# The end of a decoder layer's last product: a part order, four early weight parts, eight copies on another queue, and scalings behind a tanh

## The chip, the cores and the metric

The kernel runs on one core of a Trainium2 chip. The metric is device time of one execution in microseconds (us), the median of three runs. Engines are named as the profile names them: PE (TensorE, the matrix products), DVE (VectorE), ACT (ScalarE), POOL (GpSimd) and SP (SyncE, which here only issues transfers). SP, ACT and POOL each issue transfers on a queue of their own; the profile writes these issues as SPq, ACTq and POOLq.

## The reference

One layer of a decoder on 512 positions of width 2048, in float32. What matters for the change is its projection and its end:

```python
h = rms_norm(x, norm_g)
proj = h @ w_in                       # q, k, v, gates, u, v, z, merge logits
o_a = nsa_attention(...) * silu(z_a)  # sparse attention
o_b = spatial_gating(...) * silu(z_b)
g_a, g_b = split(sigmoid(merge_logits))
merged = g_a * (o_a @ w_up_a) + g_b * (o_b @ w_up_b)
x = x + merged @ w_out
x = x + sigmoid(x @ w_ple_gate) * (p @ w_ple)
return rms_norm(x, final_g)           # x * rsqrt(mean(x*x) + eps) * final_g
```

## The kernel before

**Products.** A large product is cut in 2 x 2 blocks and made with seven half-size products (numbered 1 to 7) of sums of blocks, not eight. Every float32 operand is split in a high and a low part, and a product of two such operands is three matmuls. The weights' high part is a cast on ACT (`high`, L181: `hs`), the low part a subtraction on DVE (`low`, L187: `ls`), and both go to rings of three tiles of 128x1024. A job is one such product on 512 columns of the weight (and the 512 that lie 1024 further on). It runs part after part; a part, written 70 or 43, is a product's number and a quarter of its depth, and it is 12 matmuls on a 128x512 weight tile. The order of the parts of the last two products (`w_out`: jobs `wo0`, `wo1`; `w_ple_gate`: jobs `pg1`, `pg0`) is a list written by hand (`LATE`).

**Around a part.** `gemm` runs for each part: first what was put off (`flush`, the list `deferred`), then `split_to`, which splits the weights one to three parts ahead (`job.lead` says how far in `pg0`) and issues the next loads, then the functions that the job's plan has for this part (`plan("pg0", 14, ...)`), then the matmuls. So every engine's order of work is the order in which this Python emits it; no scheduler moves anything.

**The last job, `pg0`.** Its parts stand in the order 10 to 13, 20, 21, 50 to 53, 22, 23, 60 to 63, 30 to 33, 70 to 73, 40 to 43. Product 4 is done by rows: for each of two row tiles t all of 40 to 43 (24 matmuls), on top of product 7's sums in PSUM, which must be copied out (L930, `keep<-ps_pg`) before product 4's first matmul overwrites them. In the profiled run part 73 is followed by product 4's first matmul at 1508.88 us. Weights of 72, 40 and 43 are split in tiles of their own (`part_place`: h0, l0, and `ob_h`); 41, 42 and 73 go through the rings.

After a block of the product comes the gate: a tanh on ACT (L970, or L1055 for product 4), `ple_add` on DVE (L963, L965), a square on ACT (L975, L1058, L1065) that adds up the rows' squares. The final norm is a multiplication by `final_g` (`weigh_x2`, L999, DVE; the weights of `final_g` are loaded by `load_fg`) and by each row's inverse root. For rows 0 and 1 the roots come from small steps on DVE (L1004 to L1010) and POOL (L1017 to L1020), for row 2 from a chain of small steps on DVE (L1004 to L1032), for row 3 from ACT's square root (after a table load at L1064). `put` scales a 128x512 block by the root (ACT L1039 for "s", DVE L1041 for "v") and sends it out (L1044).

**The merge stage** (440 to 760 us) makes the merge logits, product by product (`ps_m`), while its plan runs the gating of mixer B in `background` items (`group(g)`, eight of them). In `spatial` each group issues on ACT's queue a copy of 1 MB of `w_out` from DRAM to DRAM (`out_copies`, L1567), and on POOL's queue `add_out` adds another 1 MB to the copy before (L1522). The transfers issued by SP and ACT share eight semaphores in turn, and an engine does not issue a transfer before the transfer that had its semaphore last has landed. The logits' gate goes to DRAM from ACT (L791).

Of the kernel before, what the change touches and what calls it, by code (L numbers as in the profile page):

```python
# [13 lines left out]
F32 = mybir.dt.float32  # L14
# [24 lines left out]
class Job:  # L39
# [8 lines left out]
    def __init__(self, name, kind, w, c0, cols, kt, act, evac, banks=None, tail=0, c2=None,  # L48
                 pairs=("15", "63", "7", "24"), after=None, made=None, order=None, grown=None,
                 seq=None, adds="", lead={}):  # L50
        self.name, self.kind, self.w, self.c0, self.cols, self.kt = name, kind, w, c0, cols, kt
        self.pairs, self.after, self.made, self.order = pairs, after, made, order
        self.grown, self.plan, self.adds, self.lead = grown, {}, adds, lead
# [50 lines left out]
def kernel(ctx: ExitStack, tc: tile.TileContext, x, p, norm_g, w_in,  # L104
# [243 lines left out]
    def split_to(i, more=1):  # L348
        while state["high"] < len(subs):
            h = state["high"]  # L350
            job, k, n, ld = subs[h]
            if h > (i if job.kind == "S" else i + more):
                break
            sum_to(h)
            if job.tail and (k, n) in f_tiles:
                hi = f_tiles[k, n][:, 0:2]
            elif job.kind == "S":
                hi = quad["pool"].tile([P, 2, job.cols], F32R, tag="hs", name="hs", bufs=3)
            else:
                hi = stream.tile([P, n, job.cols], F32R, tag="hi", name="hi", bufs=4)  # L360
            src = source(h)
            {0: nc.vector.tensor_copy, 6: nc.gpsimd.tensor_copy}.get(h, high)(hi, src)
            parts[h] = [hi, None, src]
            state["high"] += 1
        sum_to(i + 1)
        while state["low"] <= min(i, len(subs) - 1):
            job, k, n, ld = subs[state["low"]]
            pt = parts[state["low"]]
            if job.tail and (k, n) in f_tiles:
                pt[1] = f_tiles[k, n][:, 2:4]  # L370
            elif job.kind == "S":
# [20 lines left out]
    def gemm():  # L392
        si = 0
        for job in jobs:
            if job.kind == "S":
# [572 lines left out]
    def gate_x2(p, cg, t, sg, src, soon=True):  # L968

        nc.scalar.activation(sg, src, AF.Tanh, scale=0.5)  # L970

        put_off = soon if callable(soon) else deferred.append if soon else later

# [3 lines left out]
        def second():  # L977
            sl = ple_add(cg, t, sg, pieces[p][t % 2])
            (soon if callable(soon) else deferred.append)(partial(square, sl))
        put_off(second)  # L980

    def final_pg(p, cg, row, ts=(0, 1)):
        other = {"3": "6", "7": "5", "2": "1"}[p]
        for t in ts:
            o = kept[other][t]
            f = partial(gate_x2, p, cg, row + t, o, o)
            if p == "3" and cg == 2:
                behind.append(partial(f, soon=behind.append))
            elif p != "2":
                (deferred.append if cg % 2 == 0 or p == "7" else later)(f)  # L990
# [55 lines left out]
    def put_row(t):  # L1046
        for cg, how in ((1, "s"), (2, "v"), (3, "s"), (0, "v")):
            put(cg, t, how=how)

    def fourth_pg(cg, t, ps):  # L1050
# [5 lines left out]
        sl = ple_add(cg, t, sg, pieces["4"][t % 2])  # L1056
        if t < TT - 1:
            nc.scalar.activation(sg, sl, AF.Square, accum_out=ss[:, t, 0:1])  # L1058
            add_squares(t, t + 1)
            inverse_root(t)  # L1060
# [463 lines left out]
    def group(g):  # L1524
# [25 lines left out]
        def second():  # L1550
            grab("z", zb_dram, "g1", 1)

        def spatial():
# [788 lines left out]
    def part_place(p, j, o):  # L2342
        f_tiles[p, j] = o()
# [55 lines left out]
```

## Time and profile before

| | |
|---|---|
| median of 3 runs | 1536.24 us (1534.26 to 1537.6) |
| the profiled execution: its own time | 1538.38 us |
| its span, first to last instruction | 1536.7 us |
| mean granted TensorE clock | 0.993 |
| PE busy | 1503.3 us (98%) |
| DVE, ACT, POOL busy | 1214.3, 854.3, 350.7 us |

The span is what the trace shows; 1.7 us of the execution's time lie around it. PE is busy nearly all the time, so only two kinds of place are of interest: the few where PE has nothing to do, and the stretch after PE's last matmul. In a timeline row, the first number is the start in us, the second the busy time, and the bracket is the engine's idle time before the row and what ended it.

### The profile page before, as it was taken

Reading aid. Unit: us, or ns where it says so; the run is one execution under the profiler, and the core shown is the slowest. Engines: PE = TensorE matmul, PEld = TensorE weight load, DVE = VectorE, ACT = ScalarE, POOL = GpSimd, SP = SyncE. Lnnn points to the kernel's source line nnn. Section 1 sums busy time; section 2 is a strip of 40 time slices with the busy share of each in tenths; the row PEclk is TensorE's granted clock in tenths of the full one; section 3 lists DMA queues with packets and bytes.
Section 4 is the critical chain, followed back from the end, with each engine's and each line's share of the span. In section 5 each row is a group of like instructions: output and inputs, shape, how many; then the busy total and the mean of one; then the engine's idle time right before and its main releaser. Section 6 shows DMA issues by size and latency. Waiting matters only on the chain.

```text
span 1536.7 us, 20290 instructions
## 1 busy us (share of the span) xinstructions
PE 1503.3 (98%) x7174; PEld 1252.3 (81%) x7174; DVE 1214.3 (79%) x1792; ACT 854.3 (56%) x1423; POOL 350.7 (23%) x507
## 2 busy tenths in 40 slices
PE   9999999999999999999999999999999999999995
PEld 8988888888888888877888888888888878877883
DVE  7787877777888787877578988968988974787677
ACT  6454445444455555544477777765555644555644
POOL 2222343321021212112223342521122111101011
PEclk9999999999999999999999999999999999999998
DMA  8897969673568898979787877678788879668682
GB/s 316 229 301 188 268 110 262 190 233 100 179 196 262 274 280 251 274 249 334 209 178 163 194 177 166 140 188 308 244 274 236 258 176 298 179 209 204 233 246 109
DMA packets 207956, 341.31 MB, mean 222 GB/s; under 512 B 30904, under 2 KB 92000, under 8 KB 206448
## 3 DMA queue, kind: packets, MB, share of 16 engines
q0 software_dynamic: 77856, 129.37, 36.8%
q1 hardware_dynamic: 111296, 161.89, 32.8%
q10 hardware_dynamic: 18704, 48.76, 8.9%
q8 instruction: 56, 0.92, 0.2%
q14 instruction: 44, 0.36, 0.1%
HBM read 284.54 MB, written 106.82 MB: 255 GB/s over the span
## 4 chain that ended last, share of the span: by engine, by line
PE 77%; DVE 8%; DMA 5%; issue 5%; ACT 3%; POOL 1%; ACTq 0%; POOLq 0%; DVEq 0%
PE ps_m L443 4%; PE ps_m L444 4%; PE ps_m L442 4%; PE ps_wo L443 2%; PE ps_wo L442 2%; PE ps_wo L444 2%; DVE ls L187 2%; PE ps_t L1774 2%; PE ps_pg L443 2%; PE ps_pg L442 2%; PE ps_pg L444 2%; PE ps_za L475 2%; PE ps_za L474 2%; PE ps_za L473 2%; PE ps_u L442 2%
## 5 line engine op out<-in xcount | busy, mean ns | idle before, releaser
L187 DVE TENSOR_TENSOR ls<-b,hs 128x1024 fp32r<-128x1024 f32 x160 | 195.8, 1224 | 101.9 <-ACT hs L181 100.8
L181 ACT CAST hs<-b 128x1024 fp32r<-128x1024 f32 x160 | 168.0, 1051 | 193.1 <-PE ps_m L444 53.8
L181 ACT CAST hs<-raw 128x1024 fp32r<-128x1024 f32 x117 | 123.1, 1052 | 132.0 <-PE ps_m L444 27.4
L187 DVE TENSOR_TENSOR ls<-raw,hs 128x1024 fp32r<-128x1024 f32 x117 | 143.2, 1224 | 39.6 <-ACT hs L181 39.2
L187 DVE TENSOR_TENSOR ls<-more,hs 128x1024 fp32r<-128x1024 f32 x94 | 115.0, 1224 | 57.8 <-ACT hs L181 57.6
L181 ACT CAST hs<-more 128x1024 fp32r<-128x1024 f32 x94 | 98.7, 1052 | 96.9 <-PE ps_wo L444 31.6
L442 PE MATMUL ps_m<-hs,act_h 128*128 128x512 f32 x256 | 100.8, 394 | 1.9 <-ACT keep L716 1.9
L443 PE MATMUL ps_m<-ls,act_h 128*128 128x512 f32 x256 | 100.4, 392 | 0.7 <-DVE ls L187 0.7
L444 PE MATMUL ps_m<-hs,act_l 128*128 128x512 f32 x256 | 100.4, 392 | 0.0
L187 DVE TENSOR_TENSOR lo<-raw,hi 128x512 fp32r<-128x512 f32 (+1 forms) x96 | 64.0, 671 | 19.7 <-PE ps_za L475 7.6
L333 DVE TENSOR_TENSOR b<-raw,b 128x1024 f32<-128x1024 f32 x64 | 78.4, 1226 | 0.6 <-DMA raw<-in_w_in_dram 0.6
L333 DVE TENSOR_TENSOR b<-b,b 128x1024 f32<-128x1024 f32 x64 | 78.1, 1220 | 0.1
L1723 ACT ACTIVATE prob<-prob,st 128x512 f32<-128x512 f32 (+3 forms) x128 | 70.8, 560 | 6.0 <-DVE st L1714 6.0
L1714 DVE CUSTOM_DVE_ANT_0 prob<-ps_s,b 128x512 f32<-128x512 f32 (+3 forms) x128 | 56.3, 487 | 13.7 <-PE ps_s L1710 13.5
L181 ACT CAST pth<-ps_t 128x512 fp32r<-128x512 f32 (+1 forms) x88 | 44.1, 547 | 35.0 <-PE ps_t L1774 34.5
L181 ACT CAST hi<-raw 128x512 fp32r<-128x512 f32 (+1 forms) x94 | 54.0, 587 | 15.1 <-PE ps_kw L474 4.0
L442 PEld LDWEIGHTS ps_m<-hs,act_h 128*128 128x128 f32 x256 | 48.5, 189 | 12.3 <-ACT keep L716 2.4
L443 PEld LDWEIGHTS ps_m<-ls,act_h 128*128 128x128 f32 x256 | 48.4, 189 | 11.0 <-DVE ls L187 1.0
L444 PEld LDWEIGHTS ps_m<-hs,act_l 128*128 128x128 f32 x256 | 48.4, 189 | 10.1
L187 DVE TENSOR_TENSOR ptl<-ps_t,pth 128x512 fp32r<-128x512 f32 (+1 forms) x88 | 52.4, 633 | 3.4 <-ACT pth L181 3.4
L473 PE MATMUL ps_za<-act_h,hi 128*128 128x512 f32 x128 | 52.3, 409 | 0.0
L473 PE MATMUL ps_q<-act_h,hi 128*128 128x512 f32 x128 | 52.1, 407 | 0.0
(692 smaller groups left out, 4535.1 us busy)
## 6 DMA issues: line engine op xcount, KB each, us to landing
raw<-in_w_in_dram SPq DMA_DIRECT2D x100, 512.0 KB, 5.4
b<-in_w_in_dram SPq DMA_DIRECT2D x64, 512.0 KB, 6.6
more<-in_w_out_dram POOLq DMA_DIRECT2D x16, 512.0 KB, 9.0
gate<-keep ACTq DMA_DIRECT2D x24, 256.0 KB, 7.6
raw<-in_w_up_b_dram SPq DMA_DIRECT2D x12, 512.0 KB, 7.9
raw<-in_w_up_a_dram SPq DMA_DIRECT2D x12, 512.0 KB, 5.3
more<-in_w_ple_gate_dram POOLq DMA_DIRECT2D x12, 512.0 KB, 7.3
raw<-in_w_out_dram SPq DMA_DIRECT2D x10, 512.0 KB, 9.7
```

Of the source, the lines that this page charges most:

```text
L181: nc.scalar.copy(hi, src)
L187: nc.vector.tensor_tensor(out=lo, in0=src, in1=hi.bitcast(F32), op=ALU.subtract)
L333: nc.vector.tensor_tensor(out=b[o], in0=b[x], in1=b[y], op=ALU.subtract)
L442: nc.tensor.matmul(o, ah, hi[:, i], start=st, stop=False, skip_group_check=go)
L443: nc.tensor.matmul(o, ah, lo[:, i], start=False, stop=False, skip_group_check=go)
L444: nc.tensor.matmul(o, al, hi[:, i], start=False, stop=sp, skip_group_check=go)
L473: nc.tensor.matmul(ps, hi[:, j], ah, start=st, stop=False)
L474: nc.tensor.matmul(ps, hi[:, j], al, start=False, stop=False)
L475: nc.tensor.matmul(ps, lo[:, j], ah, start=False, stop=sp)
L1714: nc.vector.tensor_tensor_reduce(out=pt[:, j * n:j * n + n], in0=o[:, j], in1=b0[:, 512 - n:], scale=-SLOPE[h], scalar=3.0e38, op0=ALU.add ...
L1723: nc.scalar.activation(sl, sl, AF.Exp, bias=st[:, 0, j, hh:hh + 1], scale=-1.0, accum_out=st[:, 1, j, hh:hh + 1])
L1774: nc.tensor.transpose(b[:, (2 * e + hh) * P:(2 * e + hh + 1) * P], pts[hh][:, c:c + P], ident)
```

## The change

- **Early parts.** `job.lead` goes away. A function `early_part` splits the weights of 40, 41, 42 and 43 at plan steps 18, 19, 21 and 22, each into a tile of its own (l1, h0, l0, `ob_h`); `split_to` passes over them. Part 72 goes through the rings again.
- **Final weights.** `load_fg` runs at step 10 into h1 (before: step 14 into l2), and x2's third column group is loaded at step 14 into l2 (before: step 10 into h1). Eight weighings of x move from steps 18 and 19 to steps 14 to 17, the two of column group 0 from step 20 to 18. The last pieces of the embedding (product 4's) are loaded at step 23 into kept tiles (before: step 19 into l1).
- **Gates of product 3.** The second half of the gate of column group 2 is put off by the usual list and no longer by the list `behind`, which ran it a part later.
- **Scalings.** The scalings of rows 0 and 1 are emitted in `fourth_pg`, behind the tanh of row 2, and no longer at steps 26 and 27; of each row three are now on ACT and one on DVE (before: two and two).
- **Copies.** The eight 1 MB copies of `w_out` in the merge stage are issued on SP's queue, in the item `second`, two items earlier than `spatial`. `add_out(6)` moves from the merge stage to the attention stage.

```diff
@@ split_to
-            sum_to(h)
-            if job.tail and (k, n) in f_tiles:
-                hi = f_tiles[k, n][:, 0:2]
-            elif job.kind == "S":
+            if h in parts:
+                state["high"] += 1
+                continue
+            sum_to(h)
+            if job.kind == "S":
...
+    def early_part(p, j, o):
+        i = next(n for n, sub in enumerate(subs) if sub[0].tail and sub[1:3] == (p, j))
+        src = source(i)
+        hi, lo = o[:, 0:2], o[:, 2:4]
+        high(hi, src)
+        low(hi, lo, src)
+        parts[i] = [hi, lo, src]
...
-                    split_to(si + state["ahead"] + job.lead.get(at, 0))
+                    split_to(si + state["ahead"])
@@ final_pg
             if p == "3" and cg == 2:
-                behind.append(partial(f, soon=behind.append))
+                behind.append(f)
@@ put_row
-        for cg, how in ((1, "s"), (2, "v"), (3, "s"), (0, "v")):
-            put(cg, t, how=how)
+        for cg in (1, 3, 2, 0):
+            put(cg, t, how="sv"[cg == 0])
@@ fourth_pg
         if t < TT - 1:
+            put(1, 0, how="s")
+            put(3, 0, how="s")
             nc.scalar.activation(sg, sl, AF.Square, accum_out=ss[:, t, 0:1])
+            put(0, 0)
+            put(2, 0, how="s")
+            put_row(1)
@@ group: second, spatial
             grab("z", zb_dram, "g1", 1)
+            nc.sync.dma_start(*out_copies[2 * (g % 4) + g // 4])
...
             nc.scalar.dma_start(*made_copies[n])
-            nc.scalar.dma_start(*out_copies[n])
-            if n:
+            if 0 < n < 7:
                 add_out(n - 1)
@@ add_half
-        if not i:
-            add_out(7)
+        if i < 2:
+            add_out(6 + i)
@@ load_fg
-        fg = f_tiles["fg"] = place("l2", F32).rearrange("p a s -> p (a s)")
+        fg = f_tiles["fg"] = place("h1", F32).rearrange("p a s -> p (a s)")
@@ the plan of pg0
-        t = place("l1", F32)
-        load_pieces("4", 0, lambda: [t[:, 0], t[:, 1]])
+        load_pieces("4", 0, lambda: [kept["6"][2], kept["1"][1]])
...
-    plan("pg0", 10, partial(load_x2, 2, "h1"))
+    plan("pg0", 10, load_fg)
+    plan("pg0", 14, partial(load_x2, 2, "l2"))
     plan("pg0", 14, partial(first_pg, 0))
-    plan("pg0", 14, load_fg)
...
-    plan("pg0", 19, last_pieces)
+    plan("pg0", 23, last_pieces)
     for t in range(TT):
         for cg in (1, 3):
-            plan("pg0", 18 + t // 2, partial(weigh_x2, cg, t))
+            plan("pg0", 14 + t, partial(weigh_x2, cg, t))
     for t in range(2):
-        plan("pg0", 20, partial(weigh_x2, 0, t))
+        plan("pg0", 18, partial(weigh_x2, 0, t))
...
-    plan("pg0", 18, partial(part_place, "7", 2, lambda: place("h0", F32R)))
-    plan("pg0", 20, partial(part_place, "4", 0, lambda: place("l0", F32R)))
-    plan("pg0", 22, partial(part_place, "4", 3, lambda: ob_h[:, 0:4]))
+    plan("pg0", 18, partial(early_place, "h0"), lambda: early_part("4", 0, f_tiles["l1"]))
+    plan("pg0", 19, lambda: early_part("4", 1, f_tiles["h0"]))
+    plan("pg0", 21, partial(early_place, "l0"), lambda: early_part("4", 2, f_tiles["l0"]))
+    plan("pg0", 22, lambda: early_part("4", 3, ob_h[:, 0:4]))
...
-        plan("pg0", 26 + t, partial(put_row, t))
```

The numbers of lines behind the changed places are higher by 11 to 16 in the kernel after: L963 and L965 become L974 and L976, L970 becomes L981, L975 L986, L930 L941, L999 L1010, L1039 L1050, L1041 L1052, L1055 L1066, L1058 L1071. In an order row stand the line, the operation, out<-in by name (numbers tell tiles of one name apart) and the size.

DVE in `pg0`, from about part 17 on, before: the weight lows (`ls`, and p_h for part 72), and behind the lows of the `ext` tiles the eight weighings of x in two clumps of four.

```order
L187 TENSOR_TENSOR ls<-raw,hs 128x1024 x2
L187 TENSOR_TENSOR ls<-ext,hs 128x1024 x2
L999 TENSOR_TENSOR x<-x,p_l_13252 128x512
L999 TENSOR_TENSOR x_12004<-x_12004,p_l_13252 128x512
L999 TENSOR_TENSOR x<-x,p_l_13252 128x512
L999 TENSOR_TENSOR x_12004<-x_12004,p_l_13252 128x512
L187 TENSOR_TENSOR ls<-raw,hs 128x1024
L187 TENSOR_TENSOR p_h_13338<-raw,p_h_13338 128x1024
L999 TENSOR_TENSOR x<-x,p_l_13252 128x512
L999 TENSOR_TENSOR x_12004<-x_12004,p_l_13252 128x512
L999 TENSOR_TENSOR x<-x,p_l_13252 128x512
L999 TENSOR_TENSOR x_12004<-x_12004,p_l_13252 128x512
```

DVE at the same place after, with the first low of an early part (p_l_13326, part 40) at its end:

```order
L187 TENSOR_TENSOR ls<-raw,hs 128x1024
L1010 TENSOR_TENSOR x<-x,p_h_13175 128x512
L1010 TENSOR_TENSOR x_12004<-x_12004,p_h_13175 128x512
L187 TENSOR_TENSOR ls<-raw,hs 128x1024
L1010 TENSOR_TENSOR x<-x,p_h_13175 128x512
L1010 TENSOR_TENSOR x_12004<-x_12004,p_h_13175 128x512
L187 TENSOR_TENSOR ls<-ext,hs 128x1024
L1010 TENSOR_TENSOR x<-x,p_h_13175 128x512
L1010 TENSOR_TENSOR x_12004<-x_12004,p_h_13175 128x512
L187 TENSOR_TENSOR ls<-ext,hs 128x1024
L1010 TENSOR_TENSOR p_h_13134<-p_h_13134,p_h_13175 128x512 x2
L187 TENSOR_TENSOR p_l_13326<-more,p_l_13326 128x1024
```

Each pair of weighings now stands between two lows, and all eight stand ahead of the last `ext` low.

ACT at the end of the program, from the cast of part 43's weights on, before: L930 are the copies of product 7's sums, L970 and L975 tanh and square of the block that product 7 closes, L1039 the scalings of rows 0 and 1, and L1055 the tanh of row 2.

```order
L181 CAST ob_h<-more 128x1024
L930 COPY keep_11059<-ps_pg_12976 128x512
L930 COPY keep_11060<-ps_pg_12977 128x512
L970 ACTIVATE keep_11055<-keep_11055 128x512
L970 ACTIVATE keep_11056<-keep_11056 128x512
L1039 ACTIVATE x<-x,small 128x512
L1039 ACTIVATE x_12004<-x_12004,small 128x512
L975 ACTIVATE keep_11055,small<-p_h_13175 128x512
L975 ACTIVATE keep_11056,small<-p_h_13175 128x512
L1039 ACTIVATE x<-x,small 128x512
L1039 ACTIVATE x_12004<-x_12004,small 128x512
L1055 ACTIVATE keep_11055<-ps_pg_12976 128x512
```

ACT after, from the second tanh of that block to the tanh of row 3 (the second L1066):

```order
L981 ACTIVATE keep_11056<-keep_11056 128x512
L986 ACTIVATE keep_11055,small<-p_l_13250 128x512
L986 ACTIVATE keep_11056,small<-p_l_13250 128x512
L1066 ACTIVATE keep_11055<-ps_pg_12976 128x512
L1050 ACTIVATE x<-x,small 128x512
L1050 ACTIVATE x_12004<-x_12004,small 128x512
L1071 ACTIVATE keep_11055,small<-p_h_13134 128x512
L1050 ACTIVATE p_l_13250<-p_l_13250,small 128x512
L1050 ACTIVATE x<-x,small 128x512
L1050 ACTIVATE x_12004<-x_12004,small 128x512
L1050 ACTIVATE p_l_13250<-p_l_13250,small 128x512
L1066 ACTIVATE keep_11056<-ps_pg_12977 128x512
```

The tanh of row 2 now stands ahead of all scalings, and six scalings stand between it and the tanh of row 3.

SP in the last part of the merge stage before (`b` and `raw` are 512 KB weight loads):

```order
L292 DMA raw<-in_w_in_dram 128x2x512 x8
L292 DMA b_5454<-in_w_in_dram 128x2x512
L292 DMA b_5456<-in_w_in_dram 128x2x512
L292 DMA b_5458<-in_w_in_dram 128x2x512
L292 DMA b_5507<-in_w_in_dram 128x2x512
L292 DMA b_5509<-in_w_in_dram 128x2x512
L292 DMA b_5546<-in_w_in_dram 128x2x512
L292 DMA b_5548<-in_w_in_dram 128x2x512
L292 DMA b_5591<-in_w_in_dram 128x2x512
L292 DMA raw<-in_w_in_dram 128x2x512 x8
```

SP at the same place after; of the eight copies these are the two of groups 4 and 5:

```order
L292 DMA raw<-in_w_in_dram 128x2x512 x3
L1567 DMA wo_d<-in_w_out_dram 256x1024
L292 DMA raw<-in_w_in_dram 128x2x512 x2
L1567 DMA wo_d<-in_w_out_dram 256x1024
L292 DMA raw<-in_w_in_dram 128x2x512 x3
L292 DMA b_5454<-in_w_in_dram 128x2x512
L292 DMA b_5456<-in_w_in_dram 128x2x512
L292 DMA b_5458<-in_w_in_dram 128x2x512
L292 DMA b_5507<-in_w_in_dram 128x2x512
L292 DMA b_5509<-in_w_in_dram 128x2x512
L292 DMA b_5546<-in_w_in_dram 128x2x512
L292 DMA b_5548<-in_w_in_dram 128x2x512
```

The copies now stand in one row with the weight loads.

POOL near 690 us before, where `ob_h` and `ob_l` are reloads of 2 MB and `ob_d` a store of mixer B's result:

```order
L1530 DMA mix_z<-zb_d 128x4x128
L800 DMA ob_h<-key_d 128x4096
L1522 DMA wo_d<-in_w_out_dram 256x1024
L1587 DMA ob_d<-obh 128x512
L1587 DMA ob_d<-obl 128x512
L800 DMA ob_l<-key_d 128x4096
```

POOL after:

```order
L1545 DMA mix_z<-zb_d 128x4x128
L811 DMA ob_h<-key_d 128x4096
L1602 DMA ob_d<-obh 128x512
L1602 DMA ob_d<-obl 128x512
L811 DMA ob_l<-key_d 128x4096
```

The add of 1 MB no longer stands ahead of the stores of `ob_d`.

More of the change, by code (lines that the diff above doesn't have):

```diff
@@ L49, in __init__ @@
                  pairs=("15", "63", "7", "24"), after=None, made=None, order=None, grown=None,
-                 seq=None, adds="", lead={}):
+                 seq=None, adds=""):
         self.name, self.kind, self.w, self.c0, self.cols, self.kt = name, kind, w, c0, cols, kt
         self.pairs, self.after, self.made, self.order = pairs, after, made, order
-        self.grown, self.plan, self.adds, self.lead = grown, {}, adds, lead
+        self.grown, self.plan, self.adds = grown, {}, adds
         self.seq = seq and [(p[0], int(p[1])) for p in seq.split()]
@@ L368, in split_to @@
             pt = parts[state["low"]]
-            if job.tail and (k, n) in f_tiles:
-                pt[1] = f_tiles[k, n][:, 2:4]
-            elif job.kind == "S":
+            if pt[1] is not None:
+                state["low"] += 1
+                load_next()
+                continue
+            if job.kind == "S":
                 pt[1] = quad["pool"].tile([P, 2, job.cols], F32R, tag="ls", name="ls", bufs=3)
@@ L970, in gate_x2 @@
         nc.scalar.activation(sg, src, AF.Tanh, scale=0.5)
-        put_off = soon if callable(soon) else deferred.append if soon else later
+        put_off = deferred.append if soon else later
         def square(sl):
@@ L978, in second @@
             sl = ple_add(cg, t, sg, pieces[p][t % 2])
-            (soon if callable(soon) else deferred.append)(partial(square, sl))
+            deferred.append(partial(square, sl))
         put_off(second)
@@ L1107 @@
                                        tuple(banks[at]), tail=int((n, i) == ("pg", 0)), grown=halves_of(n, w, i),
-                                       seq=LATE[at], adds="4" if (n, i) == ("pg", 0) else "64",
-                                       lead={19: 1, 20: 1, 21: 2, 22: 2, 23: 2} if (n, i) == ("pg", 0) else {})
+                                       seq=LATE[at], adds="4" if (n, i) == ("pg", 0) else "64")
             add_job(late_jobs[f"{n}{i}"])
@@ L2338, in last_pieces, with early_place @@
     def last_pieces():
-        t = place("l1", F32)
-        load_pieces("4", 0, lambda: [t[:, 0], t[:, 1]])
-    def part_place(p, j, o):
-        f_tiles[p, j] = o()
+        load_pieces("4", 0, lambda: [kept["6"][2], kept["1"][1]])
+    def early_place(tag):
+        f_tiles[tag] = place(tag, F32R)
     plan("pg0", 4, partial(load_pieces, "2", 0, kept_pieces))
     plan("pg0", 8, partial(load_x2, 0, "h2"))
-    plan("pg0", 10, partial(load_x2, 2, "h1"))
+    plan("pg0", 10, load_fg)
+    plan("pg0", 14, partial(load_x2, 2, "l2"))
     plan("pg0", 14, partial(first_pg, 0))
-    plan("pg0", 14, load_fg)
     plan("pg0", 16, partial(load_pieces, "3", 0, lambda: kept["1"]))
     plan("pg0", 17, partial(load_pieces, "7", 0, kept_pieces))
-    plan("pg0", 19, last_pieces)
+    plan("pg0", 23, last_pieces)
     for t in range(TT):
         for cg in (1, 3):
-            plan("pg0", 18 + t // 2, partial(weigh_x2, cg, t))
+            plan("pg0", 14 + t, partial(weigh_x2, cg, t))
     for t in range(2):
-        plan("pg0", 20, partial(weigh_x2, 0, t))
+        plan("pg0", 18, partial(weigh_x2, 0, t))
         plan("pg0", 23, partial(weigh_x2, 2, t))
-    plan("pg0", 18, partial(part_place, "7", 2, lambda: place("h0", F32R)))
-    plan("pg0", 20, partial(part_place, "4", 0, lambda: place("l0", F32R)))
-    plan("pg0", 22, partial(part_place, "4", 3, lambda: ob_h[:, 0:4]))
+    plan("pg0", 17, partial(early_place, "l1"))
+    plan("pg0", 18, partial(early_place, "h0"), lambda: early_part("4", 0, f_tiles["l1"]))
+    plan("pg0", 19, lambda: early_part("4", 1, f_tiles["h0"]))
+    plan("pg0", 21, partial(early_place, "l0"), lambda: early_part("4", 2, f_tiles["l0"]))
+    plan("pg0", 22, lambda: early_part("4", 3, ob_h[:, 0:4]))
     plan("pg0", 23, partial(add_squares, 0, 2))
```

## The prediction

> **What bounds the kernel now.** I read the page first, then PE's waits, then the timelines of the stretches in which PE waits or has ended.
>
> ```profile
> span 1536.7 us, 20290 instructions
> ```
>
> PE is busy for 98% of this span (the table), so time is to be had only where PE waits, runs at a lower clock, or has finished. The waits of PE over the whole span, by what ended them (total us, times, longest), name the places:
>
> ```profile
> PE ps_pg L416 <- ACT keep L930: 4.0, 1, 4.0
> ...
> PE ps_m L442 <- ACT hs L181: 2.1, 1, 2.1
> PE ps_m L442 <- ACT keep L716: 1.9, 1, 1.9
> ```
>
> The largest is ahead of product 4's first matmul; the other two stand in the merge stage. Here is PE around the first of them, part 73's first and last matmul and then product 4 (t0's first and last, t1's last):
>
> ```profile
> 1502.04 0.39 PE L442 MATMUL ps_pg<-hs,ob_l 128*128 128x512 f32 x1
> ...
> 1504.54 0.39 PE L444 MATMUL ps_pg<-hs,ob_l 128*128 128x512 f32 x1
> 1508.88 0.77 PE L416 MATMUL ps_pg<-p_l,s 128*128 128x512 f32 x1 [3.96 <-ACT keep L930]
> ...
> 1515.84 0.39 PE L418 MATMUL ps_pg<-ob_h,m_l 128*128 128x512 f32 x1
> ...
> 1521.28 0.39 PE L418 MATMUL ps_pg<-ob_h,m_l 128*128 128x512 f32 x1
> ```
>
> Full speed is (1504.54 - 1502.04) / 11 = 0.227 us a matmul. Product 4's 48 matmuls start over 12.40 us where 47 x 0.227 = 10.67 would do, so the wait of 3.96 us cost 1.73 us of clock behind it: 5.7 us together. And from PE's last start, 1521.28, to the span's end lie 15.4 us in which PE does nothing.
>
> The wait is named for an ACT copy, but ACT itself was waiting, as its timeline shows (two loads near 1493, then all that matters to the end):
>
> ```profile
> 1493.47 1.05 ACT L181 CAST p_h<-raw 128x1024 fp32r<-128x1024 f32 x1 [1.05 <-DMA raw<-pg_d]
> 1493.48 0.81 ACTq L2255 DMA_DIRECT2D p_l<-spill  x2
> ...
> 1505.36 0.63 ACT L975 ACTIVATE keep<-p_h 128x512 f32<-128x512 f32 x1 [2.46 <-DVE p_h L965]
> ...
> 1507.32 1.03 ACT L181 CAST ob_h<-more 128x1024 fp32r<-128x1024 f32 x1
> 1508.26 1.06 ACT L930 COPY keep<-ps_pg 128x512 f32<-128x512 f32 x2
> ...
> 1517.29 1.34 ACT L1039 ACTIVATE x<-x,small 128x512 f32<-128x512 f32 x2 [3.93 <-POOL small L1020]
> ...
> 1520.98 0.58 ACT L1055 ACTIVATE keep<-ps_pg 128x512 f32<-128x512 f32 x1
> 1523.05 0.63 ACT L1058 ACTIVATE keep<-p_h 128x512 f32<-128x512 f32 x1 [1.49 <-DVE p_h L965]
> ```
>
> ACT sat 2.46 us for DVE's p_h (a square), and only behind that came the cast of part 43 and the copies. DVE, from 1478.90 on:
>
> ```profile
> 1478.90 1.23 DVE L187 TENSOR_TENSOR ls<-raw,hs 128x1024 fp32r<-128x1024 f32 x1 [1.50 <-ACT hs L181]
> 1480.04 0.69 DVE L963 SCALAR_TENSOR_TENSOR keep<-keep,keep 128x512 f32<-128x512 f32 x1
> ...
> 1482.69 1.22 DVE L187 TENSOR_TENSOR ls<-raw,hs 128x1024 fp32r<-128x1024 f32 x1
> 1485.99 1.23 DVE L187 TENSOR_TENSOR ls<-raw,hs 128x1024 fp32r<-128x1024 f32 x1 [2.08 <-ACT hs L181]
> ...
> 1489.73 1.23 DVE L187 TENSOR_TENSOR ls<-ext,hs 128x1024 fp32r<-128x1024 f32 x1 [1.37 <-ACT hs L181]
> 1490.87 2.49 DVE L999 TENSOR_TENSOR x<-x,p_l 128x512 f32<-128x512 f32 x4
> 1493.28 1.22 DVE L187 TENSOR_TENSOR ls<-raw,hs 128x1024 fp32r<-128x1024 f32 x1
> ...
> 1508.38 1.23 DVE L187 TENSOR_TENSOR ob_h<-more,ob_h 128x1024 fp32r<-128x1024 f32 x1 [0.59 <-ACT ob_h L181]
> 1509.53 1.29 DVE L999 TENSOR_TENSOR p_h<-p_h,p_l 128x512 f32<-128x512 f32 x2
> ...
> 1521.59 0.69 DVE L963 SCALAR_TENSOR_TENSOR keep<-keep,p_l 128x512 f32<-128x512 f32 x1 [0.24 <-ACT keep L1055]
> ...
> 1523.80 0.16 DVE L1004 TENSOR_REDUCE small<-small 128x1 f32<-128x4 f32 x1 [0.79 <-ACT keep L1058]
> ...
> 1527.14 0.69 DVE L963 SCALAR_TENSOR_TENSOR keep<-keep,p_l 128x512 f32<-128x512 f32 x1
> ```
>
> DVE sat idle for 1.50, 2.08 and 1.37 us up to 1489.73, and then has no bracket until 1508.38. The clumps of weighings (L999) stand in that full stretch, so the gates' second halves (L963, L965), squares, copies and PE are late by DVE's work, not by PE's or ACT's own.
>
> **The tail, step by step.** Unit prices from start to start: a low 1.14 (1478.90 to 1480.04), a weighing 2.41 / 4 = 0.60 (1490.87 to 1493.28), a step of a gate's second half 2.65 / 4 = 0.66 (1480.04 to 1482.69).
>
> 1. *DVE up to part 73's low.* In the new order of DVE, from the low at 1478.90 through the low of 73, there are 10 lows, 10 weighings, 8 gate steps and product 3's two sums from PSUM (two 128x512 operations, taken as weighings): 11.4 + 6.0 + 5.3 + 1.2 = 23.9, without an idle gap, since each pair of weighings fills one: end at 1502.8, and the result seen about 0.1 later. PE needs this low for the second matmul of part 73, 1502.04 + 0.23 = 1502.27. So I charge PE **0.7 us** of waiting at part 73 (a new, smaller wait; between 0 and 4.1, below). The order leans on ACT's casts being there: the low at 1489.73 waited for its cast, and DVE now comes to that low at 1490.95, 1.2 later, so the cast has that much room.
> 2. *PE.* Part 73 ends at 1505.6 instead of 1504.9. The copies are free of their old cover: the squares need gate steps that end near 1500.4, so ACT is done with them by 1502.6 and with part 43's cast by 1503.6; the copy of t0 (0.53) can run as soon as part 73's first six matmuls are done, before the other six are. So product 4 starts at once, at full speed: 47 x 0.227 + 0.39 = 11.1, end **1516.7** against 1521.67: -5.0. t0 ends at 1511.3. The two issues of the moved pieces' loads stand ahead of the copies on ACT; at 1493.48 such a pair ran beside a cast that started at 1493.47, so they cost 0 to 0.8 and I take 0.
> 3. *The roots of rows 0 and 1.* Behind low 73 DVE has two lows and two weighings (3.5) and then the small steps (the weighing pair at 1509.53 to POOL's start took 2.06, of which 1.2 are the pair): 1502.8 + 3.5 + 0.9 = 1507.2. POOL started at 1511.59 and let ACT go at 1517.29, 5.70 later:
>
> ```profile
> 1511.59 0.55 POOL L1017 TENSOR_TENSOR small<-small 128x2 f32<-128x2 f32 x1 [32.70 <-DVE small L1010]
> ```
>
> So the roots are there at 1512.9, -4.4.
> 4. *Row 2.* DVE subtracts (1.2), ACT's tanh of the first block (0.62) is out at 1508.5, four gate steps end at 1511.2, the squares at 1512.1 (two in turn, the second behind DVE's last step). ACT then takes row 2's tanh, 1512.1 to 1512.7, instead of 1520.98: it no longer stands behind four scalings that waited 3.93 us for POOL. DVE's step L963 for it comes at 1512.7 instead of 1521.59: **-8.9**. ACT meanwhile does two scalings (1512.9 to 1514.3), then row 2's square (1523.05 before, now 1514.3: -8.7).
> 5. *Row 3.* DVE's chain for row 2 came 0.75 behind the square and took from 1523.80 to 1527.14, 3.34, before L963 of row 3. Now: 1514.3 + 0.75 + 3.34 = 1518.4, if the tanh of row 3 is done. That one stands behind four more scalings on ACT: 1515.1 + 4 x 0.66 + 0.6 = 1518.3. So both meet, and L963 comes at 1518.4 instead of 1527.14: -8.7. What is behind it (square, ACT's root, last scalings and stores) is unchanged. What is late next is DVE's chain for row 2, no longer POOL's roots, and PE's end is 1.0 us off the path.
>
> The tail gives **-8.7**. If low 73 is in time it is up to 0.7 more. Of the loads that are swapped, `final_g` has the less room: asked for at step 10 and read from step 14, four parts or 4 x 12 x 0.227 = 10.9 us later, and it took 8.9 in the trace, so it lies beside PE with 2.0 to spare:
>
> ```profile
> p_l<-in_final_g_dram ACTq DMA_DIRECT2D x1, 1024.0 KB, 8.9
> ```
>
> x2's third quarter, of the same size, is asked for at step 14 and first read by the gate of product 3, past step 20. The two scalings that move from DVE to ACT are in the steps above.
>
> **The merge stage.** PE from the later of the two waits on:
>
> ```profile
> 715.97 0.50 PE L442 MATMUL ps_m<-hs,act_h 128*128 128x512 f32 x1 [1.94 <-ACT keep L716]
> ...
> 717.38 0.63 PE L444 MATMUL ps_m<-hs,act_l 128*128 128x512 f32 x1
> ...
> 720.37 0.45 PE L442 MATMUL ps_m<-hs,act_h 128*128 128x512 f32 x1
> ```
>
> ACT's idle time behind both waits:
>
> ```profile
> 673.25 1.04 ACT L181 CAST hs<-b 128x1024 fp32r<-128x1024 f32 x1 [7.06 <-issue]
> ...
> 714.82 0.62 ACT L181 CAST sobh<-sob 128x512 fp32r<-128x512 f32 x1 [5.08 <-DMA ob_d<-obh]
> ```
>
> And the transfers from 640 to 720 us (count, KB each, median us from issue to landing):
>
> ```profile
> raw<-in_w_in_dram SPq DMA_DIRECT2D x8, 512.0 KB, 14.1
> ...
> wo_d<-in_w_out_dram POOLq DMA_DIRECT2D x2, 1024.0 KB, 17.8
> ...
> wo_d<-in_w_out_dram ACTq DMA_DIRECT2D x2, 1024.0 KB, 20.3
> ...
> ob_d<-obh POOLq DMA_DIRECT2D x1, 256.0 KB, 12.8
> ```
>
> First, the wait at 715.97: ACT sat 5.08 us for a store of `ob_d` on POOL's queue, which took 12.8 us for 256 KB. It stood behind the 1 MB add (L1522), two of which took 17.8 in the median. The change takes that add out of the row. Then ACT's copy is no longer late, and PE gains the 1.94 us and what the clock lost behind it: 7 matmuls from 717.38 to 720.37 took 2.99 where 1.59 would do, 1.4 us. Together -3.3.
>
> [...]
>
> Second, the wait of 2.1 us near 674: ACT sat 7.06 us because its store of the gate had its semaphore from a weight load of SP's queue, which landed late. After the change the copy of 1 MB stands in this row of semaphores; the copies on ACT's queue took 20.3 us here, weight loads 14.1. So this stall stays and may grow by up to 20.3 - 14.1 = 6.2 of landing; it may also go, -2.1 and 1.4 of clock. PE felt 2.1 of 7.06, a third; a third of 6.2 is 2.1, and since the copy is issued some us earlier than before I take **+1.8**.
>
> Third, weight loads behind a copy in SP's row can land later, by 0 to 6.2 for each copy; loads that took 14.1 in the median made PE wait only where the rows say, so they are asked for early, and I take 0. Bounds for the stage: -4.0 - 2 x 1.4 = -6.8 if both waits go, +6.2 if neither goes and one load is late in full. Taken: -3.3 + 1.8 = **-1.5**.
>
> **Sum.** -8.7 - 1.5 = -10.2. Against the profiled execution, 1536.7 + 1.7 around it = 1538.4, that is 1528.2; this execution stands 2.1 above the median of the runs, and I carry that over: 1536.2 - 10.2 = **1526.0**.
>
> **Rivals.**
> - *The copies hold up SP's row (slower).* Place: the merge stage. A weight load behind a 1 MB copy waits until the copy is through, its split is late, PE waits. For: transfers are crowded there, and loads take 14.1 us already. Against: the lead with which they are asked for. Price: up to 6.2 us of PE for a copy. The gain of 10.2 and the 0.2% more (3.1 us, about what a measurement of this kernel can tell from no change) are gone with 13.3 us of waiting, so it decides from three of the eight copies: 1526.0 + 18.6 = 1544.6, chance 0.06. With two, 1538.4, within 0.2%: 0.05. [...]
> - *The casts hold DVE as before.* If the idle times before the lows of 1485.99 and 1489.73 stay and the weighings only come on top, DVE is 2.08 + 1.37 = 3.45 late at 73, PE waits there for 4.1, and the roots and all behind them shift alike: the tail gives -5.2 and the sum 1529.5. For: those idle times ended with casts, which wait for ring tiles that PE frees. Against: the casts have 1.2 us of room, as worked out. 0.18.
> - *The wait ahead of product 4 does not go*, since ACT cannot issue the two loads of pieces ahead of its copies until an earlier transfer has landed, as at 673.25, where 7.06 went. ACT is free at 1503.6, and the first copy is needed 1.1 later, so PE would lose 6.0 and 1.4 or more of clock, and the sum is -2.8: 1533.4. Against: by then the program's last weights are in. 0.05.
> - *The merge stage gives more.* Both waits go with the clock behind them: -8.7 - 6.8 = -15.5, 1520.7. For: both were ended by transfers that move. Against: the first has its semaphore from a queue that gets longer. 0.14.
>
> **The numbers.** My forecast has 0.52, with a range of its own of 3 us to each side. From 1520 to 1532.5 lie it, the held DVE and the larger merge stage; left out are the slower cases and the wait that stays, 0.16, and the edges of the others. Faster by over 0.2% (below 1533.1): 0.52 + 0.18 + 0.14 + half of 0.05 = 0.865; within it 0.05 and the other half, 0.075; slower 0.06.
>
> **What would show it.** Right: no wait of PE ahead of product 4 and one under 1.5 us at part 73; its 48 matmuls over 11.1 us; DVE without an idle bracket from 1478 to about 1507; row 2's tanh ahead of POOL's end; the last L963 about 13 us after PE's part 73; no ACT stall near 715, an ACT stall of 7 us or more near 674. Wrong: PE waits named for DVE's lows at parts 70 to 72 (the weighings came too early), a wait of PE in the merge stage named for a weight load, or ACT late for row 3's tanh by more than 1 us.

## The result and the profile after

| | before | after |
|---|---|---|
| median | 1535.32 us (1534.26 to 1537.6, 4 runs) | 1524.16 us (1522.85 to 1525.83, 4 runs) |
| span of the profiled execution | 1536.7 us | 1521.1 us |
| ratio after / before | | 0.9926, 95% interval 0.9909 to 0.9943 |

The change takes 11.2 us off the median; 1526.0 was forecast, 10.2 below the median of the three runs known then and 9.3 below this one. The two profiled executions lie 15.6 us apart, more than the medians, since the one of before was 3 us above its median and the one of after 1.3 below. Where they differ is seen from the same matmul in both traces. PE's waits, again as total us, times and longest:

```profile
PE ps_t L1789 <- DVE ptl L187: 1.9, 4, 0.8
PE ps_m L453 <- ACT hs L181: 1.7, 1, 1.7
...
PE ps_pg L454 <- DVE ls L187: 1.1, 2, 0.6
...
PE ps_m L454 <- DVE ls L187: 0.8, 1, 0.8
```

The wait ahead of product 4 (L427 now) is gone, the one for `keep` in the merge stage too, and the pair near 672 us is there still, 1.7 and 0.8. Of the 1.1 us at L454 half is the new wait at part 73. PE at the end of the program:

```profile
1494.04 0.39 PE L453 MATMUL ps_pg<-hs,ob_l 128*128 128x512 f32 x1
1494.92 0.50 PE L454 MATMUL ps_pg<-ls,ob_l 128*128 128x512 f32 x1 [0.49 <-DVE ls L187]
...
1497.32 0.39 PE L455 MATMUL ps_pg<-hs,ob_l 128*128 128x512 f32 x1
1497.55 0.39 PE L427 MATMUL ps_pg<-p_l,s 128*128 128x512 f32 x1
...
1508.20 0.39 PE L429 MATMUL ps_pg<-ob_h,m_l 128*128 128x512 f32 x1
```

Part 73 begins at 1494.04, 8.0 us earlier than before: that much came from the stages ahead. It waits 0.49 us for its low; product 4 follows without a wait and takes 10.65 us from first to last start. DVE, whose clumps of weighings the prediction took for the cause:

```profile
1470.90 1.23 DVE L187 TENSOR_TENSOR ls<-raw,hs 128x1024 fp32r<-128x1024 f32 x1 [1.50 <-ACT hs L181]
1472.04 1.29 DVE L1010 TENSOR_TENSOR x<-x,p_h 128x512 f32<-128x512 f32 x2
...
1475.90 1.22 DVE L187 TENSOR_TENSOR ls<-raw,hs 128x1024 fp32r<-128x1024 f32 x1
1477.03 1.29 DVE L1010 TENSOR_TENSOR x<-x,p_h 128x512 f32<-128x512 f32 x2
1478.24 1.22 DVE L187 TENSOR_TENSOR ls<-raw,hs 128x1024 fp32r<-128x1024 f32 x1
1479.37 1.28 DVE L1010 TENSOR_TENSOR x<-x,p_h 128x512 f32<-128x512 f32 x2
1480.58 1.22 DVE L187 TENSOR_TENSOR ls<-ext,hs 128x1024 fp32r<-128x1024 f32 x1
...
1493.65 1.22 DVE L187 TENSOR_TENSOR ls<-raw,hs 128x1024 fp32r<-128x1024 f32 x1
...
1503.85 0.69 DVE L1010 TENSOR_TENSOR p_l<-p_l,p_h 128x512 f32<-128x512 f32 x1 [0.19 <-ACT keep L986]
```

The brackets of 2.08 and 1.37 us are gone: after 1470.90 no row of DVE has an idle bracket until 1503.85, and the weighings (L1010) stand between the lows. ACT at the end:

```profile
1496.44 0.59 ACT L941 COPY keep<-ps_pg 128x512 f32<-128x512 f32 x1 [1.01 <-PE ps_pg L455]
1497.80 0.59 ACT L941 COPY keep<-ps_pg 128x512 f32<-128x512 f32 x1 [0.78 <-PE ps_pg L455]
...
1503.72 0.58 ACT L1066 ACTIVATE keep<-ps_pg 128x512 f32<-128x512 f32 x1
1506.23 1.34 ACT L1050 ACTIVATE x<-x,small 128x512 f32<-128x512 f32 x2 [1.93 <-POOL small L1031]
1507.48 0.61 ACT L1071 ACTIVATE keep<-p_h 128x512 f32<-128x512 f32 x1
...
1509.93 0.70 ACT L1050 ACTIVATE p_l<-p_l,small 128x512 f32<-128x512 f32 x1
1510.54 0.57 ACT L1066 ACTIVATE keep<-ps_pg 128x512 f32<-128x512 f32 x1
```

The tanh of row 2 (the first L1066) comes ahead of the scalings (L1050), which waited 1.93 us for POOL; row 3's (1510.54) begins as the last of six scalings ends. From part 73's first matmul to the last landing the trace before has 34.6 us, this one 27.05: **-7.5**. Between the 2001st and the 3601st matmul, which enclose the merge stage, they have 360.7 and 353.7: **-7.0**.

### The profile page after: what moved, and what is told of

Same layout as the page of the kernel before. It is cut to its first block, busy times and chain, and to the rows that moved or that the text cites. A ratio compares the mean times of both kernels' runs of the same rounds, so it can differ in the third digit from the quotient of the medians.

```text
span 1521.1 us, 20288 instructions
## 1 busy us (share of the span) xinstructions
PE 1497.0 (98%) x7174; PEld 1249.0 (82%) x7174; DVE 1212.3 (80%) x1790; ACT 856.2 (56%) x1425; POOL 351.7 (23%) x507
## 4 chain that ended last, share of the span: by engine, by line
PE 83%; DVE 8%; DMA 3%; ACT 2%; issue 2%; POOL 1%; ACTq 0%; POOLq 0%; DVEq 0%
PE ps_m L454 6%; PE ps_m L455 6%; PE ps_m L453 6%; DVE ls L187 3%; PE ps_wo L454 2%; PE ps_wo L453 2%; PE ps_wo L455 2%; PE ps_t L1789 2%; PE ps_pg L454 2%; PE ps_pg L453 2%; PE ps_pg L455 2%; PE ps_za L486 2%; PE ps_za L485 2%; PE ps_za L484 2%; PE ps_u L453 2%
## 5 line engine op out<-in xcount | busy, mean ns | idle before, releaser
L454 PE MATMUL ps_m<-ls,act_h 128*128 128x512 f32 x256 | 99.6, 389 | 0.0
L455 PEld LDWEIGHTS ps_m<-hs,act_l 128*128 128x128 f32 x256 | 48.1, 188 | 10.1
L454 PEld LDWEIGHTS ps_m<-ls,act_h 128*128 128x128 f32 x256 | 48.1, 188 | 9.8
```

The lines of the kernel that those rows point to most:

```text
L454: nc.tensor.matmul(o, ah, lo[:, i], start=False, stop=False, skip_group_check=go)
L455: nc.tensor.matmul(o, al, hi[:, i], start=False, stop=sp, skip_group_check=go)
```

## The experiments

Eleven runs followed, one of them (`e_again`) of the changed kernel itself. Times are medians; "end" is the time from part 73's first matmul to the last landing, and "merge" the time between the 2001st and 3601st matmul, both of the one trace. Before each stands in a row of its own for the trace shown above.

| kernel | median us | before beside it | ratio (95%) | merge | end |
|---|---|---|---|---|---|
| before | 1535.32 | | | 360.7 | 34.57 |
| changed | 1524.16 | 1535.32 | 0.9926 (0.9909 to 0.9943) | 353.7 | 27.05 |
| e_copies | 1535.19 | 1535.52 | 0.9996 (0.9987 to 1.0005) | 356.3 | 34.52 |
| e_add | 1531.73 | 1535.52 | 0.9978 (0.9969 to 0.9987) | 354.9 | 34.64 |
| e_tail | 1527.56 | 1535.52 | 0.9949 (0.9936 to 0.9962) | 356.6 | 27.02 |
| e_scal | 1531.74 | 1535.52 | 0.9976 (0.9967 to 0.9985) | 359.5 | 31.43 |
| e_noscal | 1527.76 | 1534.93 | 0.9951 (0.9939 to 0.9964) | 355.5 | 30.10 |
| e_weigh | 1532.76 | 1534.93 | 0.9983 (0.9974 to 0.9992) | 357.8 | 31.86 |
| e_noweigh | 1527.05 | 1534.93 | 0.9950 (0.9937 to 0.9962) | 353.4 | 26.98 |
| e_two | 1523.56 | 1534.93 | 0.9926 (0.9912 to 0.9939) | 357.7 | 25.53 |
| e_again | 1524.42 | 1536.49 | 0.9926 (0.9914 to 0.9939) | 353.4 | 27.04 |
| e_gate | 1520.66 | 1536.49 | 0.9903 (0.9890 to 0.9917) | 351.8 | 27.24 |
| e_best | 1519.55 | 1536.49 | 0.9898 (0.9883 to 0.9914) | 350.9 | 25.66 |

The end repeats within 0.1 us where it is the same code (34.52 to 34.64; 27.02 to 27.05). The merge stage does not: 356.6 to 360.7 in the four traces whose merge stage is that of before, 353.4 to 357.7 in the five with the changed one. That scatter is why two single traces gave 15.6 us and the medians 11.2. A part of it has a place: in the eleven traces that have the wait near 674 us it was 1.1 to 3.0 us long. The granted clock of 660 to 680 us was 0.91 in the traces of before and `e_add` and 1.00 in those of the changed kernel, `e_copies`, `e_tail`, `e_scal` and `e_again`. The wait of 3.0 is that of `e_two`, where the mean clock of the whole execution was 0.995, against 0.997 in `e_again`.

**The copies alone.**

```diff
             grab("z", zb_dram, "g1", 1)
+            nc.sync.dma_start(*out_copies[2 * (g % 4) + g // 4])
...
             nc.scalar.dma_start(*made_copies[n])
-            nc.scalar.dma_start(*out_copies[n])
```

> The kernel before, with nothing but the eight 1 MB copies on SP's queue. Theory A (each of the merge stage's waits has its own transfer): the wait near 716 us is the add on POOL's queue, so it stays with its lost clock, and only the wait near 516 may go: 0 to -2 us, about 1534.5. Theory B (the copies on ACT's queue crowd all other transfers): the wait near 716 goes too, -4 us or more, about 1531. Rival of the prediction (copies hold up SP's loads): a wait for a weight load appears, slower.

No change that can be measured. ACT's idle time near 711 us stayed, with the same name:

```profile
710.86 0.62 ACT L181 CAST sobh<-sob 128x512 fp32r<-128x512 f32 x1 [4.34 <-DMA ob_d<-obh]
```

PE's wait for `keep` is there too, 1.2 us, and the store of `ob_d` took 12.1 us to land (12.8 before). So theory B falls: it is not the copies on ACT's queue that made the store late. The rival by which they would hold up SP's row falls too, as far as PE's time goes.

**The add alone.**

```diff
-            if n:
+            if 0 < n < 7:
                 add_out(n - 1)
...
-        if not i:
-            add_out(7)
+        if i < 2:
+            add_out(6 + i)
```

> The kernel before, with nothing but the add of the seventh copy moved from the merge stage to the attention stage. Theory A: ACT no longer waits for the store of ob_d near 716 us, PE's 1.9 us and the 1.4 to 1.7 us of clock behind it come back: -3.5 us, about 1532. Theory B: the store is late from the copies, the wait stays: 0.

3.8 us less (2.0 to 4.8 by the interval), as theory A has it, and the store of `ob_d` landed after 6.7 us. No wait for `keep` is left in the merge stage; these are PE's waits there, of the whole span's:

```profile
PE ps_m L442 <- ACT hs L181: 1.1, 1, 1.1
...
PE ps_m L443 <- DVE ls L187: 0.8, 1, 0.8
```

**The end alone.** The changed kernel, with copies and add put back:

```diff
-            nc.sync.dma_start(*out_copies[2 * (g % 4) + g // 4])
...
+            nc.scalar.dma_start(*out_copies[n])
-            if 0 < n < 7:
+            if n:
                 add_out(n - 1)
...
-        if i < 2:
-            add_out(6 + i)
+        if not i:
+            add_out(7)
```

> The changed kernel with copies and add as before, so only the changes at the end are in. If the two traces are right in their parts (end -7.6 us, merge stage -6.9), this stands 7 to 8 us below before, about 1527.5, and 3.5 us above the changed kernel. If the merge stage's difference was mostly one of the two executions that were profiled, this is as fast as the changed kernel, 1524 to 1525.

8.0 us below before, and 3.1 to 3.4 above the changed kernel in its two series: the end and the add together are the whole gain (8.0 + 3.8 = 11.8 against 11.2 to 12.1), and the copies' move is worth nothing that these runs can tell.

**The scalings alone, and taken back.** This is `e_scal`, in the kernel before; `e_noscal` is the same edit the other way round, in the changed kernel.

```diff
-        for cg, how in ((1, "s"), (2, "v"), (3, "s"), (0, "v")):
-            put(cg, t, how=how)
+        for cg in (1, 3, 2, 0):
+            put(cg, t, how="sv"[cg == 0])
...
+            put(1, 0, how="s")
+            put(3, 0, how="s")
             nc.scalar.activation(sg, sl, AF.Square, accum_out=ss[:, t, 0:1])
+            put(0, 0)
+            put(2, 0, how="s")
+            put_row(1)
...
-        plan("pg0", 26 + t, partial(put_row, t))
```

> The kernel before, with nothing but the scalings of rows 0 and 1 behind the tanh of row 2 (three on ACT, one on DVE). PE's wait of 4 us ahead of product 4 stays. By the prediction's step 4 the tanh of row 2 then comes at the end of t0's matmuls, 1516.3 instead of 1521.0, and row 2's square about 4 us earlier: -4 us, about 1531. The rival: POOL's roots (1517.3) bound all that follows, and less than 1 us comes of it.

> The changed kernel with the scalings of rows 0 and 1 at their old place and shared two and two. The wait ahead of product 4 is still gone, but on ACT the tanh of row 2 stands again behind four scalings that wait for POOL's roots (1506.2 in the changed kernel's trace): 1510.4 instead of 1503.7, row 2's square about 5 us later. Expected +4 to +5 us over the changed kernel, about 1528.5. The rival (the end is bound by DVE's order, the scalings' place is worth little once DVE is early): +1 or less, 1525.

Alone they gave 3.8 us (the end 3.1 shorter) with PE's wait of 3.9 still there; taken back out of the changed kernel they cost 3.6 (the end 3.05 longer), a little under the 4 to 5 expected. They are a part of their own that does not need PE's wait to go.

**The weighings alone, and taken back.** For `e_weigh`, in the kernel before:

```diff
-        fg = f_tiles["fg"] = place("l2", F32).rearrange("p a s -> p (a s)")
+        fg = f_tiles["fg"] = place("h1", F32).rearrange("p a s -> p (a s)")
...
-    plan("pg0", 10, partial(load_x2, 2, "h1"))
+    plan("pg0", 10, load_fg)
+    plan("pg0", 14, partial(load_x2, 2, "l2"))
-    plan("pg0", 14, load_fg)
...
-            plan("pg0", 18 + t // 2, partial(weigh_x2, cg, t))
+            plan("pg0", 14 + t, partial(weigh_x2, cg, t))
...
-        plan("pg0", 20, partial(weigh_x2, 0, t))
+        plan("pg0", 18, partial(weigh_x2, 0, t))
```

For `e_noweigh`, in the changed kernel, the weighings alone:

```diff
-            plan("pg0", 14 + t, partial(weigh_x2, cg, t))
+            plan("pg0", 18 + t // 2, partial(weigh_x2, cg, t))
...
-        plan("pg0", 18, partial(weigh_x2, 0, t))
+        plan("pg0", 20, partial(weigh_x2, 0, t))
```

> The kernel before, with nothing but final_g loaded first, x2's third quarter after it, and the ten weighings moved into DVE's idle times (parts as before, scalings as before). If DVE's idle times were the cause of the late end, DVE is 3.5 us earlier, PE's wait ahead of product 4 falls from 4.0 to about 0.5, the clock behind it stays up, and the end comes 3 to 4 us earlier: about 1532. The rival (the early splits of parts 40 to 43 take away the wait): the wait stays near 4 us, 0 to -1 us.

> The changed kernel with the ten weighings at their old steps 18 to 20 (early parts, loads and scalings as changed). If the weighings in DVE's idle times carry the gain, DVE is 3 to 4 us late at the lows of parts 70 to 73, PE waits there for 3 to 4 us in all, and the time is 3 to 4 us over the changed kernel: 1527.5 to 1528. The rival (early parts carry it): within 1 us of the changed kernel.

Alone: 2.2 us less by the medians and the end 2.7 shorter, a little under what was expected, PE's wait down to 1.2, and product 4 near full speed (10.79 us). Without them, the changed kernel loses 2.9, and not at the end (26.98) but ahead of it; PE's waits of that trace:

```profile
PE ps_pg L454 <- DVE ls L187: 2.8, 3, 1.9
```

The longest of the three is at 1493.26, for the low of a part before 73, and the mean clock of that execution was 0.996, where the changed kernel's had 0.997; on DVE the idle times of 2.08 and 1.37 us are back. Product 4 follows part 73 without a wait in this trace too. So the moved weighings alone take the wait ahead of product 4 from 4.0 to 1.2 us, and the rest of the change takes it away even without them, but then PE waits for DVE's lows a few parts earlier. What removes the last 1.2 us, the early splits, the swapped loads or the gates of product 3, is not shown: none of them was run alone.

**Shorter roots.**

```diff
-        for n, (s, c) in enumerate(((-0.703952253, 1.68191391), (-0.5, 1.5), (-0.5, 1.5))):
+        for n, (s, c) in enumerate(((-0.703952253, 1.68191391), (-0.5, 1.5))):
...
-            tt(out=v if n == 2 else y, in0=y, in1=q, op=ALU.mult)
+            tt(out=v if n == 1 else y, in0=y, in1=q, op=ALU.mult)
```

> The changed kernel with two of POOL's three Newton steps for the roots of rows 0 and 1 (8 instead of 12 POOL instructions; the third step's refinement is left out). POOL took 7.1 us for the 12 in the changed kernel and ACT waited 1.9 us for it; with 8 the roots come 2.4 us earlier, row 2's square is then bound by DVE's gate step (1505.9) and comes 1.6 us earlier, and all behind it: -1.5 us, about 1522.6. The rival (PE's end or the tanh of row 3 behind six scalings on ACT bounds the end): 0 to -0.5.

The end is 1.52 shorter, as expected, and ACT's scalings no longer wait (no bracket at the first L1050):

```profile
1508.80 0.58 ACT L1066 ACTIVATE keep<-ps_pg 128x512 f32<-128x512 f32 x1
1509.28 1.32 ACT L1050 ACTIVATE x<-x,small 128x512 f32<-128x512 f32 x2
1510.98 0.64 ACT L1071 ACTIVATE keep<-p_h 128x512 f32<-128x512 f32 x1 [0.38 <-DVE p_h L976]
```

The medians moved by 0.6 only and the ratios are alike, so by whole times this gain is not shown; the merge stage's scatter is larger. `e_best` and `e_gate` below have the same 1.6 between their ends (25.66 and 27.24).

**The gate's stores on POOL's queue, alone, with the shorter roots, and the changed kernel beside them.**

```diff
-            deferred.append(lambda: nc.scalar.dma_start(gate_dram[n][block(t, c0 + c)], o))
+            deferred.append(lambda: nc.gpsimd.dma_start(gate_dram[n][block(t, c0 + c)], o))
```

> The changed kernel with the gate's 24 stores issued on POOL's queue. If ACT's stall near 670 us is its gate store waiting for a weight load of SP's queue to land (6.7 us of ACT, 1.7 + 0.8 of PE in the changed kernel's trace), the casts no longer stand behind that store, PE's two waits there go, and the time falls by about 2.5 us, to 1521.7. The rival (the weight load itself is late and PE waits for it anyway): the waits stay, now for a cast behind a load, 0. POOL's row gets longer: an ob_d or sob_d store that is late behind a gate store would show as a new wait of ACT, +1 to +3.

> The changed kernel with both: gate stores on POOL's queue and two Newton steps for the roots of rows 0 and 1 (the third step's refinement is left out). If both parts hold, -2.5 and -1.5: about 1520.2. If only the shorter root does: 1522.6.

> The changed kernel again, for the same chip as the two above and a second trace of its merge stage. If the stage's time scatters from execution to execution, as seven traces of other kernels suggest (353.4 to 357.7 us between the same two matmuls in kernels with the changed merge stage), this trace differs from the first (353.7) by 1 us or more while its end from part 73 on repeats 27.05 us within 0.1; the median is 1524.2 within 1 us.

`e_gate` is 3.8 us below the changed kernel of the same series, more than the 2.5 expected, and PE's wait for `hs` in the merge stage is gone; its waits begin:

```profile
PE ps_t L1789 <- DVE ptl L187: 2.0, 3, 1.1
PE ps_spin L1211 <- POOL eps_t L126: 1.4, 1, 1.4
PE ps_pg L454 <- DVE ls L187: 1.1, 2, 0.6
```

`e_best` is 4.9 below, 1519.55 us, 0.9898 of before (0.9883 to 0.9914): it beats both kernels, though its roots are without their last refinement. `e_again` repeated the end within 0.01, and, against what was expected, the merge stage too (353.4 after 353.7).

## Why the prediction was right, point by point

- *Part 73's low* (0.7 us of waiting): 0.49, and 0.79 over full speed from part 73's first matmul to product 4's (3.51 against 2.72). The count of DVE's rows held: from the low at 1470.90 to the end of 73's low 24.0 us, forecast 23.9.
- *Product 4 without a wait, full speed:* 10.65 us from first to last start, forecast 10.67.
- *The roots, -4.4:* this step was mis-sized. POOL started 5.08 us after part 73's first matmul (forecast 5.16), but took 7.11 us, not the 5.70 of the trace before, so the roots came only 3.1 earlier. That put row 2's square 13.4 behind part 73's first matmul where the forecast had 12.3, and DVE's chain behind it: the tail gave -7.5 and not -8.7. `e_two` shows POOL on the path: with four of its twelve steps left out the end is 1.52 shorter.
- *Row 2's tanh ahead of the scalings:* 9.7 behind that matmul, forecast 10.1. Shown by `e_scal` and `e_noscal`.
- *The wait near 716, -3.3 with its clock:* it was the add, and the size was right; `e_add` has it alone, -3.8. Whether the add held the store by standing ahead of it on POOL's queue, as the prediction has it, or by its traffic is open: a weight load on SP's queue at that time (issued at 697.39 before, at 694.64 in `e_add`) fell from 14.5 to 9.3 us as well.
- *The stall near 674, +1.8:* the term that was wrong. ACT's stall stayed, 6.67 us for 7.06, and did not grow; PE's 1.7 + 0.8 were 2.1 + 0.8 before:

```profile
670.79 0.33 ACTq L802 DMA_DIRECT2D gate<-keep  x1
671.21 1.04 ACT L181 CAST hs<-b 128x1024 fp32r<-128x1024 f32 x1 [6.67 <-DMA b<-in_w_in_dram]
```

  The bracket names a weight load (b): issued at 657.21 on SP's queue, it took 13.5 us to land, at 670.7, and the store that had its semaphore next was issued at 670.79. The copy did come into this row of semaphores, one store ahead, but it had been issued at 650.74 and took 12.4 us and not the 20.3 of the copies on ACT's queue, so it landed before it could hold ACT up:

```profile
wo_d<-in_w_out_dram SPq DMA_DIRECT2D x1, 1024.0 KB, 12.4
```

  That the stall was this store is shown by `e_gate`. Without the 1.8 the merge stage's term is -3.3, and the medians of the changed kernel and `e_tail` differ by 3.1 to 3.4.
- With -7.5 and -3.3 the sum is -10.8 for -10.2: the errors of 1.2 and 1.8 went opposite ways, so part of the nearness is luck. The time itself came out 1.8 below the forecast, about half of it because a fourth run lowered the median of before from 1536.24 to 1535.32.
- *Rivals:* neither the held-up row of SP nor a stall ahead of the copies of product 7 showed. The casts did not hold DVE either, since its two idle times went. Of the larger merge stage one of the two waits went and the other stayed; that the two traces are 7.0 us apart there is in part the stage's scatter. In `e_copies` no wait of PE is named for a weight load; that none was delayed is not shown (from 640 to 720 us the loads of `raw` took 15.2 us in the median, 14.1 before).

## What to carry to other kernels

When an engine waits, follow the row of waits back to one that was busy without a break and look for its idle time some microseconds earlier: work moved there shortened a wait two engines away (from 4.0 to 1.2 us in `e_weigh`; moved back, in `e_noweigh`, it cost 2.9). One gate store on ACT's queue that waited for a transfer of SP's held up ACT's casts behind it for 6.67 us, and with these stores on POOL's queue the time fell by 3.8 (`e_gate`): such a store belongs on a queue whose engine has nothing urgent. And where one stage's time scatters by 4 us, compare single traces stage by stage, and whole times by medians alone.

## What the runs showed of the hardware

POOL's small steps (128x2) ran at two speeds. Before, the last of them ran while DVE had nothing to do, from 1515.53 to 1517.29; of the twelve in the trace before, the fifth to the eighth and the twelfth:

```profile
1514.34 0.53 POOL L1017 TENSOR_TENSOR small<-small 128x2 f32<-128x2 f32 x1
1514.94 0.65 POOL L1018 TENSOR_TENSOR small<-small 128x2 f32<-128x2 f32 x1
1515.68 0.19 POOL L1019 TENSOR_SCALAR small<-small 128x2 f32<-128x2 f32 x1
1515.95 0.20 POOL L1020 TENSOR_TENSOR small<-small 128x2 f32<-128x2 f32 x1
...
1517.06 0.20 POOL L1020 TENSOR_TENSOR small<-small 128x2 f32<-128x2 f32 x1
```

After, DVE was busy nearly throughout, and of the twelve the same ones read:

```profile
1501.87 0.52 POOL L1028 TENSOR_TENSOR small<-small 128x2 f32<-128x2 f32 x1
1502.47 0.65 POOL L1029 TENSOR_TENSOR small<-small 128x2 f32<-128x2 f32 x1
1503.21 0.51 POOL L1030 TENSOR_SCALAR small<-small 128x2 f32<-128x2 f32 x1
1503.80 0.20 POOL L1031 TENSOR_TENSOR small<-small 128x2 f32<-128x2 f32 x1
...
1506.01 0.20 POOL L1031 TENSOR_TENSOR small<-small 128x2 f32<-128x2 f32 x1
```

0.19 to 0.20 us with DVE idle, 0.5 to 0.7 beside DVE's 128x512 operations of 0.68 to 0.69 us (L963 and L965 before, L974, L976 and L1010 after); the two of 0.20 in the trace after begin in DVE's only two breaks (0.19 us ahead of 1503.85, 0.36 ahead of 1506.24). The starts agree: they lie 0.27 to 0.28 us apart beside the idle DVE, 0.59 to 0.77 beside the busy one. DVE's operations kept their length: L974 and L976 took 0.68 to 0.69 us beside POOL's steps, and 0.69 each from 1511.57 on, when POOL had ended. What ties the two engines is not shown. A price taken from a trace in which the neighbour rests is not the price beside a busy one (5.70 us for the twelve before, 7.11 after).

The clock behind a short wait is not fixed by the wait. Near 674 us, PE waited twice in each of four kernels. The stretch from 660 to 680 us of the kernel before and of the changed kernel, with PE's granted clock in the third column from the end:

```profile
660.00:680.00 20.00, 17.12 (x69) 13.46 (x68) 12.42 (x14) 7.54 (x10) 3.41 (x5) 0.91 1.02 329
660.00:680.00 20.00, 17.52 (x78) 13.96 (x77) 13.15 (x15) 8.73 (x12) 3.41 (x5) 1.00 0.93 299
```

The same of `e_copies`:

```profile
660.00:680.00 20.00, 17.59 (x78) 13.97 (x77) 13.08 (x15) 8.75 (x12) 3.40 (x5) 1.00 0.96 306
```

And of `e_add`:

```profile
660.00:680.00 20.00, 18.10 (x73) 14.24 (x72) 13.07 (x14) 7.72 (x11) 3.41 (x5) 0.91 1.00 336
```

Waits of 1.7 + 0.8 (changed, `e_copies`) left the clock at 1.00, and 1.1 + 0.8 (`e_add`) brought it to 0.91, as 2.1 + 0.8 had before. So the prediction's 1.4 us of clock behind a 1.94 us wait was right as a reading and is no rule by itself. In the trace before, PE ran at half speed behind each of its three longest waits (2.1, 1.9 and 4.0 us), each time for 3.41 us, from 676.10, 717.06 and 1508.95 us on. Why 1.1 + 0.8 cost clock and 1.7 + 0.8 did not is not shown here.
